# A list schedule that models VectorE's and GpSimd's shared SBUF ports and later DMA landings

## The chip, the cores and the metric

One Trainium2 chip, one core. The time is the device time of one execution in microseconds (us), the median of several runs. A run with the hardware profiler on gives the trace from which all durations here are read. The engines are called by the profile's names: PE (TensorE), PEld (its weight loads), DVE (VectorE), ACT (ScalarE), POOL (GpSimd) and SP (SyncE, which issues nearly all DMAs here).

## The reference

One layer over 4096 tokens of width 1024, batch 1. A normalised and modulated `h` feeds three groups of heads: sliding-window attention, RWKV-7 (a state that is updated token by token) and GLA (gated linear attention in chunks). Each is multiplied by its SiLU gate, and one output projection follows.

```python
h = _rmsnorm(x, g_pre) * (1.0 + scale[:, None]) + shift[:, None]
proj = h @ w_in
aq, ak, av, ag, rkv, rg, gq, gkk, gv, gg = jnp.split(proj, ...)
attn = _sliding_window_attention(...) * jax.nn.silu(ag)
rwkv = _rwkv7_mixer(...) * jax.nn.silu(rg)
gla = _gla_mixer(...) * jax.nn.silu(gg)
y = jnp.concatenate([attn, rwkv, gla], axis=-1) @ w_out
return x + gate[:, None] * _rmsnorm(y, g_post)
```

## The kernel before

The tokens are worked off in 16 chunks of 256. Weights and activations are split into a high and a low float16 part, and a projection sums three products.

**Phase 1** (from about 100 us to 1000 us of the span) runs, for each chunk: loading and normalising `x` (tiles `xh`, `xt`, `rsx`, `rb`, and the transposed activations `hT`); the projections into the PSUM tiles `pv`, `lp`, `zz`, `gqk`, through two banks that they share in turn; GLA (`qb`, `op`, `osb`, and the transposes `ot`); and RWKV. RWKV's inner triangular solve goes through small 32x32 matmuls (`Xp`, `Xq`, `X2`), its state update through a loop of four steps a chunk: `rp` on PE, a copy `rs` on DVE, `up` on PE, two copies into `UV` on ACT, `sp` on PE, and `Ss`, `Sst` on DVE. Its output `yp` is copied to `ysb`, normalised (statistics `bst`, `mv` and the small `ve` on DVE; the power `yr`, the subtraction `ysb<-ysb,mv` and the product `ysb<-ysb,yr` on POOL) and transposed (`yt`). Beside it the weights of the later phase are read in pieces `cs`, split into `ch` by ACT and DVE and written to DRAM; POOL also works out the gate's adaLN row (`gaw`, `gacc`) and masks (`ATm`).

**Phase 2** (to the end) runs the attention's projections (`kp`, `qp`, `vp`), the gates (`gp`), attention (`sc`, `pr`, `pT`, `ovp`) and the output projection, in seven products a chunk (`op`). Four of the seven weight blocks stay in SBUF (`o1`, `o4`, `o5`, `o6`); three are streamed through one tile `ov` in halves. The result `yv` gets the residual added from `x2`, whose transfer shows as `x<-in_x`.

**What sets the order.** Each operation goes through a `Lane`, which calls the real engine at line 339 (so every row of the profile carries that line) and tells an `Order` about it. `Order.note` (from line 100) records for each operation a `Step`: its engine, how long it holds the engine (`occ`), when its result is there (`lat`), and what it needs. `Order.pin` (from line 225) then does a list schedule over all recorded steps of a phase: it takes the engine that can start first, picks among that engine's ready steps the one of the lowest rank (about the order in which the program emitted it), with an exception on PE that avoids changing the array's tiling, puts it at the earliest time that the model allows, and ties it behind the last step of that engine. The model decides nothing but the order on each engine; on the chip each engine then works its queue off in that order and waits at its head for whatever is not there. `pin` is called twice, once after phase 1 and once after phase 2. The steps between (the first projections of phase 2) are left to the framework's own priorities.

In that model DVE and POOL are independent, and a DMA's result is there 1.9 to 4.8 us after its issue, by size (the line with `(8, 1.9), (32, 2.0), ...`).

Of the kernel before, what the change touches and what calls it, by code (L numbers as in the profile page):

```python
# [35 lines left out]
URGENT = 150  # L36
HOME = {('kp', 'mq'): 'tr', ('cw', 'm'): 'at'}
TILING_WAIT = 0.6
LANES = ((0.06, 1.04e-3, VL), (0.02, 1.0e-3, AL), (0.1, 2.3e-3, 0.0), (0.0, 1e-3 / 2.4, PL), (0.05, 0.0, 2.0))

SIZE = {F16: 2, BF16: 2, F32: 4, I32: 4}
# [17 lines left out]
class Step:  # L59


    __slots__ = ("ins", "eng", "occ", "lat", "table", "array", "bytes", "half", "rank", "needs", "turn", "start", "end", "then", "joint")


class Order:
# [34 lines left out]
    def note(self, eng, name, outs, ins, func, r):  # L100

        st = Step()
        st.ins, st.eng, st.table, st.array, st.bytes, st.then = r.ins, str(eng.engine).split(".")[-1], None, None, 0, []
        st.joint = self.joint
        st.half, st.rank = None, len(self.steps) + self.lag
        e, o = st.eng, outs[0]
        on_psum = [a for a in ins if str(a.tensor.space) == "PSUM"]
        n = max(math.prod(a.shape[1:]) for a in [o, *ins[:1]])
        cols = len([a for a in ins[1:] if math.prod(a.shape[1:]) == 1]) if n > 1 else 0
        if e == "PE":  # L110
            f32, lhs = ins[0].dtype == F32, self.region(ins[0])
            n = math.prod(o.shape[1:])
            _, p0, p1, _ = self.region(o)
            rows, cs = (lhs[1] // 32, (lhs[2] + 31) // 32), (p0 // 32, (p1 + 31) // 32)
            rows, cs = [(0, 4) if b - a > 2 else (a, b) for a, b in (rows, cs)]
            mode = (rows[1] - rows[0], cs[1] - cs[0])
            took = n * (2 if f32 else 1) / 2400 + 0.003
            took = max(took, 0.056 if not f32 else 0.0 if mode[1] < 4 else 0.109 if n > 16 else 0.21)
            issue = 0.017 if f32 and mode == (1, 2) else 0.009 if f32 and mode[0] == 1 else 0.007
            cells = [4 * a + b for a in range(*rows) for b in range(*cs)]  # L120
            st.array = (mode, cells, 2 if f32 and name == "matmul" else 1, took, issue)
            st.occ = st.lat = 0.0
        elif e == "SP":
            st.bytes = math.prod(ins[0].shape) * SIZE[ins[0].dtype]
            kb = st.bytes / 1024
            st.occ = 0.47
            st.lat = next((t for k, t in ((8, 1.9), (32, 2.0), (128, 2.3), (256, 2.6), (512, 3.5)) if kb <= k), 4.8)
        elif e == "Activation":
            st.occ = (0.05 if on_psum else 0.093) + 0.093 * (len(ins) - 1) + 0.832e-3 * n
            st.lat = st.occ + 0.1  # L130
            if len(outs) > 1:
                st.occ += 0.187
                st.lat = st.occ + 0.02
            st.table = LN_TABLE if func == AF.Ln else EXP_TABLE if func in (AF.Exp, AF.Tanh) else None
        elif e == "Pool":
            if name == "memset":
                st.occ = 0.06
            elif name == "tensor_copy":
                st.occ = 0.25 if n <= 2 else 0.11 + 0.95e-3 * n
            elif n <= 8:  # L140
                st.occ = 0.33 + 0.165 * n
            else:
                st.occ = 0.42 + 1.5e-3 * n if n <= 512 else 1.85e-3 * n
            st.lat = st.occ + 0.05
        else:
            if name == "tensor_reduce":
                n = math.prod(ins[0].shape[1:])
            fast = name in ("tensor_scalar", "tensor_single_scalar") and not on_psum and o.dtype == F32
            fixed, rate = 0.065 + 0.06 * (cols > 0), 1.04e-3
            if fast:  # L150
                rate = 0.53e-3
            elif name == "transpose":
                fixed = 0.09
            elif name == "tensor_tensor_scan":
                rate = 2.08e-3
            elif name == "memset":
                fixed, rate = 0.05, 0.3e-3
            elif name == "tensor_tensor" and len(o.shape) == 3 and o.shape[2] <= 16 and n > 16:
                fixed, rate = 0.09, 1.55e-3
            st.occ = fixed + rate * n  # L160
            st.lat = st.occ + 0.085

        k, st.needs, st.turn = len(self.steps), {}, []
        out_r, in_r = [self.region(a) for a in outs], [self.region(a) for a in ins]
        if e in ("Activation", "DVE"):

            st.half = (out_r[0][1], in_r[0][1] if e == "Activation" and in_r and out_r[0][2] - out_r[0][1] <= 64 else None)
        tiles = {a.tensor.name: a.tensor for a in [*outs, *ins]}

        if e == "SP" and self.behind is not None:  # L170
            st.turn.append(self.behind)

        def need(j, data=False):
            st.needs[j] = st.needs.get(j, False) or data

        for t, tensor in tiles.items():
            if t not in self.known:
                self.known.add(t)
                if t in self.held and tensor.tag:
                    held = self.slots.setdefault((tensor.owner_uid, tensor.tag), [])  # L180

                    if held and self.users.get(held[-1]):
                        st.turn.append(self.users[held[-1]][0])
                    if len(held) == self.held[t]:
                        for j in self.users.get(held.pop(0), ()):
                            need(j)
                    held.append(t)
            elif t in self.held and self.users.get(t):
                st.turn.append(self.users[t][0])
            if str(tensor.space) == "PSUM":  # L190
                for j in self.users.get(t, ()):
                    need(j)

        def meet(a, b):
            return a[1] < b[2] and b[1] < a[2] and (a[3] is None or a[3] & b[3])

        def covered(a, b):
            return b[1] <= a[1] and a[2] <= b[2] and (a[3] is None or not a[3] & ~b[3])

        for a in in_r:  # L200
            for w, j in self.wrote.get(a[0], ()):
                if meet(a, w):
                    need(j, True)
        for a in out_r:
            if a[3] is not None:
                for old in (self.wrote, self.read):
                    for w, j in old.get(a[0], ()):
                        if meet(a, w):
                            need(j)
                    old[a[0]] = [(w, j) for w, j in old.get(a[0], ()) if not covered(w, a)]  # L210
            self.wrote.setdefault(a[0], []).append((a, k))
        for a in in_r:
            self.read.setdefault(a[0], []).append((a, k))
        for t in tiles:
            self.users.setdefault(t, []).append(k)
        st.needs.pop(k, None)
        self.steps.append(st)
# [7 lines left out]
    def pin(self):  # L225

        steps = self.steps
# [16 lines left out]
                ready[st.eng][k] = 0.0  # L244
        free = dict.fromkeys(ENGINES, 0.0)
        cells, mode, table, pipe, half = [0.0] * 16, None, None, 0.0, {}
        last, count = {}, 0
        while count < len(steps):
            e = min((e for e in ENGINES if ready[e]), key=lambda e: max(free[e], min(ready[e].values())))
            now = max(free[e], min(ready[e].values())) + 1e-9  # L250
            at = sorted((k for k, t in ready[e].items() if t <= now), key=lambda k: (steps[k].rank, k))
            k = at[0]
            if e == "PE" and mode is not None and steps[k].array[0] != mode:

                same = [q for q in at if steps[q].array[0] == mode]
                wait = max(now - ready[e][q] for q in at if steps[q].array[0] != mode)
                if same and (mode != (4, 4) or wait < TILING_WAIT):
                    k = same[0]
            first = max(free[e], ready[e].pop(k))
            for k in bursts.get(k, [k]):  # L260
                st, t = steps[k], max(first, free[e])
                if e == "PE":
                    m, at, passes, took, issue = st.array
# [7 lines left out]
                else:  # L271
# [3 lines left out]
                            t = max(t, free[e] + 0.115)  # L275
                    if st.table is not None and st.table != table:
                        t, table = max(t, free[e] + 1.28), st.table
                    free[e], st.end = t + st.occ, t + st.lat
                    if st.bytes:

# [1918 lines left out]
```

## Time and profile before

| | us |
|---|---|
| median of 3 runs | 1997.24 (1992.85 to 1998.64) |
| the profiled execution | 1996.2 |
| its span in the trace | 1994.4 |

The span is divided by the engines' work. Over it PE is busy 94%, DVE 72%, ACT 56%, POOL 19%, and almost all of POOL's work is in phase 1. A row of the wait view reads: engine and tile that waited, what released it, then the sum in us, how many times, and the longest. A row of the timeline reads: start, duration, engine, operation, output and inputs, count, and in brackets the idle time before it with its releaser. A row of the grouped view ends in the group's busy time, the mean of one in ns, and the idle time before it.

### The profile page before, as it was taken

The numbers are of one execution on the slowest core, as the hardware profiler recorded it, in microseconds if no ns is written. First come the engines' busy times: TensorE is split into PE (matmuls) and PEld (weight loads), VectorE is DVE, ScalarE is ACT, GpSimd is POOL, SyncE is SP. The second block draws the span as 40 slices with busy tenths as digits, with TensorE's granted clock in tenths as the row PEclk, the third lists the DMA queues.
The fourth block names the chain that finished last, engine by engine and source line by source line (L and its number), as shares of the span: only waits on it lengthen the run. The fifth ranks groups of instructions, "written<-read, shape, count | busy, mean of one in ns | idle before, by whom it ended". The sixth has DMA issues, their size and how long they took to land.

```text
span 1994.4 us, 59065 instructions
## 1 busy us (share of the span) xinstructions
PE 1882.8 (94%) x24651; PEld 1453.4 (73%) x24651; DVE 1427.5 (72%) x3919; ACT 1115.0 (56%) x2529; POOL 373.1 (19%) x549
## 2 busy tenths in 40 slices
PE   5799989999999999999999999999999999999997
PEld 1677777777777777777776677876778767787793
DVE  4877877788877888777647776667666676666766
ACT  4877878677786676565435443344434444434443
POOL 0623223543223454223200000000000000000001
PEclk8999999999999999999999999999999999999999
DMA  9345544443342433125234433344333443334315
GB/s 373 128 152 179 155 140 125 148 139 109 105 133 88 125 111 111 61 65 185 77 132 142 151 109 112 109 146 130 109 110 109 149 130 109 100 117 151 110 47 181
DMA packets 154261, 257.55 MB, mean 129 GB/s; under 512 B 49026, under 2 KB 100994, under 8 KB 147844
## 3 DMA queue, kind: packets, MB, share of 16 engines
q1 hardware_dynamic: 153844, 253.19, 39.7%
q8 instruction: 195, 3.19, 0.7%
q14 instruction: 78, 0.64, 0.1%
q10 hardware_dynamic: 144, 0.52, 0.1%
HBM read 192.83 MB, written 60.82 MB: 127 GB/s over the span
## 4 chain that ended last, share of the span: by engine, by line
PE 55%; DVE 23%; DMA 9%; ACT 6%; issue 4%; POOL 1%; SPq 1%; ACTq 0%; DVEq 0%; POOLq 0%
PE gp L339 16%; PE op L339 11%; PE qp L339 5%; PE zz L339 4%; PE pv L339 2%; PE kp L339 2%; PE ovp L339 2%; PE lp L339 2%; DVE mtp L339 2%; DVE q L339 2%; PE sc L339 2%; DVE tsc L339 1%; SPq L339 1%; PE gqk L339 1%; DMA ov<-woscr 1%
## 5 line engine op out<-in xcount | busy, mean ns | idle before, releaser
L339 PEld LDWEIGHTS <-mtp 128*128 128x128 f16 x1344 | 128.7, 98 | 144.9 <-issue 9.2
L339 ACT ACTIVATE pr<-pr,nm,lsc 128x160 f32<-128x160 f32 (+2 forms) x256 | 129.0, 506 | 101.8 <-DVE nm L339 101.7
L339 PE MATMUL op<-o,mtp 128*128 128x512 f16 x768 | 182.2, 379 | 1.9 <-DVE yv L339 1.7
L339 PE MATMUL op<-ov,mtp 128*128 128x512 f16 x576 | 140.8, 379 | 4.4 <-DMA ov<-woscr 4.4
L339 PEld LDWEIGHTS <-hT 128*128 128x128 f16 x1536 | 117.6, 99 | 24.0 <-ACT hT L339 3.9
L339 ACT ACTIVATE ag<-gp,gh 128x512 f32<-128x512 f32 x64 | 43.9, 686 | 158.8 <-PE gp L339 158.8
L339 POOL TENSOR_TENSOR ry<-sy,expo 128x1 f32<-128x1 f32 x30 | 17.7, 606 | 584.7 <-DVE sy L339 584.7
L339 DVE SCALAR_TENSOR_TENSOR ag<-ag,gp 128x512 f32<-128x512 f32 x64 | 43.7, 683 | 103.1 <-ACT ag L339 103.1
L339 DVE TENSOR_TENSOR yv<-op,yv 128x512 f32<-128x512 f32 x105 | 72.1, 688 | 59.0 <-PE op L339 39.6
L339 PE MATMUL pv<-gvh,hT 128*128 128x272 f16 x512 | 98.2, 284 | 6.3 <-ACT hT L339 3.8
L339 PE MATMUL zz<-hT,kh 128*128 128x256 f16 x512 | 93.0, 274 | 0.0
L339 PE MATMUL zz<-hT,rh 128*128 128x256 f16 x512 | 92.5, 277 | 0.1
L339 PE MATMUL lp<-hT,Lh 128*128 128x256 f16 x512 | 91.7, 273 | 0.3 <-ACT vg L339 0.3
L339 PE MATMUL gqk<-hT,gqkh 128*128 128x256 f16 x512 | 87.9, 273 | 3.4 <-DVE zb L339 3.3
L339 DVE CUSTOM_DVE_ANT_0 pr<-sc,ab,kept 128x160 f32<-128x160 f32 (+2 forms) x256 | 83.1, 375 | 10.7 <-PE sc L339 10.2
L339 PE MATMUL gp<-hT,q4h 128*128 128x256 f16 x512 | 90.1, 276 | 0.0
L339 PE MATMUL qp<-hT,q1h 128*128 128x256 f16 x512 | 87.0, 275 | 0.9 <-DVE kT L339 0.9
L339 PE MATMUL qp<-hT,q0h 128*128 128x256 f16 x512 | 86.3, 273 | 0.5 <-issue 0.5
L339 PE MATMUL zz<-hT,vh 128*128 128x256 f16 x512 | 86.3, 273 | 0.0
L339 PE MATMUL gp<-hT,q3h 128*128 128x256 f16 x512 | 85.3, 273 | 0.0
L339 PE MATMUL gp<-hT,q5h 128*128 128x256 f16 x512 | 85.1, 273 | 0.0
L339 PE MATMUL gp<-hT,q6h 128*128 128x256 f16 x512 | 85.0, 273 | 0.0
(429 smaller groups left out, 5736.6 us busy)
## 6 DMA issues: line engine op xcount, KB each, us to landing
ov<-woscr SPq DMA_DIRECT2D x96, 512.0 KB, 4.5
xh<-in_x SPq DMA_DIRECT2D x32, 512.0 KB, 4.4
xt<-in_xc SPq DMA_DIRECT2D x16, 1024.0 KB, 8.2
hscr<-hT SPq DMA_DIRECT2D x16, 1024.0 KB, 5.0
hT<-hscr SPq DMA_DIRECT2D x16, 1024.0 KB, 5.0
x<-in_x SPq DMA_DIRECT2D x30, 512.0 KB, 4.2
out<-yv SPq DMA_DIRECT2D x30, 512.0 KB, 2.9
cs<-in_w SPq DMA_DIRECT2D x56, 256.0 KB, 3.6
```

The source lines that it names most:

```text
L339: r = f(*args, **kw)
```

## The change

The recorded step gets a flag `port`. On DVE it is set when no input is in PSUM and the operation either reads two tensors (elementwise, scan, scalar_tensor_tensor) or is a tensor_scalar or copy of at least 32 elements a partition. On POOL it is set when the operation is wider than 8 elements a partition. `pin` keeps one time `held`: a flagged step on either engine starts no earlier than `held`, and sets it to its own end. If the step that an engine would take is flagged and the ports are held for over 0.3 us more, the first ready step without the flag is taken instead. Beside that, the table of DMA landings is raised. No operation is added, removed or altered: on each engine the same instructions stand in another order, 65 table loads on ACT among them, as before.

```diff
+SWAP = 0.3
...
-            st.lat = next((t for k, t in ((8, 1.9), (32, 2.0), (128, 2.3), (256, 2.6), (512, 3.5)) if kb <= k), 4.8)
+            st.lat = next((t for k, t in ((8, 2.0), (32, 2.2), (128, 2.8), (256, 3.7), (512, 4.6)) if kb <= k), 5.2)
...
+        wide = max([math.prod(a.shape[1:]) for a in [*outs, *ins]])
+        if e == "DVE":
+            two = len(ins) > 1 and name in ("tensor_tensor", "tensor_add", "tensor_sub", "tensor_mul", "tensor_tensor_scan",
+                                            "scalar_tensor_tensor")
+            st.port = not on_psum and (two or wide >= 32 and name in ("tensor_scalar", "tensor_single_scalar", "tensor_copy"))
+        else:
+            st.port = e == "Pool" and wide > 8
...
+            if steps[k].port and held > now + SWAP:
+                k = next((q for q in at if not steps[q].port), k)
...
+                    if st.port:
+                        t = max(t, held)
+                        held = t + st.occ
```

Of the 18648 matmuls on PE, 9126 stand ahead of phase 2's first projection before and 9062 after; the number of times that neighbouring matmuls there differ in array tiling is 540 before and 538 after. Three places follow.

**ACT, around the evacuation of `pv` in the tenth chunk.** `vg` is GLA's value tile, `ch<-cs` a pass over a piece of the output weights that was just loaded, `xt` and `hT` belong to the next chunk's normalisation. Before:

```order
L339 ACTIVATE vg_9077<-pv_9079,ivgv_252 128x256
L339 ACTIVATE vg_9077<-pv_9079,ivgk1_253 128x16
L339 ACTIVATE ch_9295,wo_ss_99<-cs_9183 128x512
L339 ACTIVATE ch_9371,wo_ss_99<-cs_9297 128x512
L339 ACTIVATE vg_9077<-pv_9147,ivgv_252 128x256
L339 ACTIVATE vg_9077<-pv_9147,ivgk1_253 128x16
L339 ACTIVATE ch_9431,wo_ss_99<-cs_9373 128x512
L339 ACTIVATE ch_9490,wo_ss_99<-cs_9433 128x512
```

Of the change:

```order
L352 ACTIVATE vg_9077<-pv_9079,ivgv_252 128x256
L352 ACTIVATE vg_9077<-pv_9079,ivgk1_253 128x16
L352 ACTIVATE xt_9306<-xt_9306,sh_74,gs_73 128x256 x3
L352 ACTIVATE hT_9421<-xt_9306 128x512
L352 ACTIVATE vg_9077<-pv_9147,ivgv_252 128x256
L352 ACTIVATE vg_9077<-pv_9147,ivgk1_253 128x16
L352 ACTIVATE xt_9306<-xt_9306,sh_74,gs_73 128x256 x2
L352 ACTIVATE hT_9421<-xt_9306 128x512
```

The passes over loaded weights moved back, and the next chunk's normalisation moved ahead of them.

**PE, around GLA's transposes `ot` of the eleventh chunk.** `zz` with `vh`, `vl` is the twelfth chunk's third RWKV projection; `gqk` is the projection after it, and `pv` with `hT_11429` is the thirteenth chunk's. Before:

```order
L339 LDWEIGHTS vh_264
L339 MATMUL zz_11933<-hT_10329,vh_264 128x256
L339 MATMUL ot_11955<-first_63,osb_11762 128x128 x4
L339 LDWEIGHTS vl_265
L339 MATMUL zz_11933<-hT_10329,vl_265 128x256
```

Of the change:

```order
L352 MATMUL pv_12198<-gvh_250,hT_11429 128x272
L352 MATMUL kp_12071<-first_63,KB_11095 128x128 x4
L352 LDWEIGHTS hT_11429
L352 MATMUL pv_12273<-gvh_250,hT_11429 128x272
L352 LDWEIGHTS hT_11429
L352 MATMUL pv_12273<-gvl_251,hT_11429 128x272
L352 MATMUL ot_11955<-first_63,osb_11762 128x128 x4
```

`ot` moved back behind the rest of `zz`, all of `gqk` and the first half of the thirteenth chunk's `pv`. Counted from the chunk's last `op` matmul, 46 full-array projection matmuls stood ahead of `ot` before and 90 stand there now.

**PE in phase 2, at a streamed weight block.** `op_20386` uses the streamed tile `ov`, whose second half is loaded apart from the first; `op_20518` is the next product, with the resident block `o4`. Before:

```order
L339 MATMUL op_20386<-ov_17806,mtp_17818 128x512
L339 LDWEIGHTS mtp_17818
L339 MATMUL op_20518<-o4_17804,mtp_17818 128x512
L339 LDWEIGHTS mtp_17818
L339 MATMUL op_20386<-ov_17806,mtp_17818 128x512
```

Of the change:

```order
L352 MATMUL op_20386<-ov_17806,mtp_17818 128x512
L352 LDWEIGHTS mtp_17818
L352 MATMUL op_20518<-o4_17804,mtp_17818 128x512
L352 LDWEIGHTS mtp_17818
L352 MATMUL op_20518<-o4_17804,mtp_17818 128x512
```

Between the two halves of `ov` one matmul of the next product stood, now eight do. This repeats in each chunk of the steady part. The order at the last chunk, where `ov` is also streamed, is the same in both.

More of the change, by code (lines that the diff above doesn't have):

```diff
@@ L59 @@
 class Step:
-    __slots__ = ("ins", "eng", "occ", "lat", "table", "array", "bytes", "half", "rank", "needs", "turn", "start", "end", "then", "joint")
+    __slots__ = ("ins", "eng", "occ", "lat", "table", "array", "bytes", "half", "rank", "needs", "turn", "start", "end", "then", "joint", "port")
 class Order:
@@ L246, in pin @@
         cells, mode, table, pipe, half = [0.0] * 16, None, None, 0.0, {}
-        last, count = {}, 0
+        last, count, held = {}, 0, 0.0
         while count < len(steps):
```

## The prediction

> **What bounds the kernel now.** I read the page first, then the engines' work by stretches, then PE's waits in each stretch, and last a few microseconds of the timeline where PE waited longest.
>
> ```profile
> span 1994.4 us, 59065 instructions
> PE 55%; DVE 23%; DMA 9%; ACT 6%; issue 4%; POOL 1%; SPq 1%; ACTq 0%; DVEq 0%; POOLq 0%
> 0.00:100.00 100.00, 66.03 (x426) 39.30 (x430) 64.28 (x193) 67.44 (x124) 34.80 (x58) 0.90 0.68 250
> 100.00:1000.00 900.00, 859.48 (x13730) 690.43 (x13722) 713.18 (x2152) 622.36 (x1344) 304.44 (x441) 1.00 0.39 122
> 1000.00:1950.00 950.00, 926.02 (x10364) 710.17 (x10363) 622.80 (x1526) 411.49 (x1038) 27.90 (x45) 1.00 0.38 121
> 1950.00:1994.40 44.40, 31.30 (x143) 13.55 (x141) 27.21 (x49) 13.73 (x25) 6.01 (x6) 0.94 0.50 171
> ```
>
> The second row is the chain of waits by engine; the others are stretches with the busy time of PE, PEld, DVE, ACT and POOL. PE sets the pace in both phases: it is idle 900.00 - 859.48 = 40.5 us in phase 1 and 950.00 - 926.02 = 24.0 us in phase 2. An order cannot shorten PE's own work, and the tiling changes stay at 540 against 538, so those 64.5 us bound what the change can win from 100 to 1950 us. POOL, whose ports the change models, works 304.44 us in phase 1 and 27.90 in phase 2: the port part of the change is a matter of phase 1. The first 100 us (34 idle on PE) wait for the first transfers, and PE's order differs little there; I count nothing. So the question is which of PE's waits go, and which come.
>
> ```profile
> PE ot L339 <- DVE osb L339: 5.3, 5, 1.6
> PE gqk L339 <- DVE zb L339: 3.3, 4, 1.3
> PE Xq L339 <- DVE Xs L339: 3.1, 3, 1.7
> PE yt L339 <- POOL ysb L339: 2.6, 1, 2.6
> PE ktp L339 <- DVE bon L339: 2.6, 4, 1.1
> PE vp L339 <- DVE zb L339: 1.8, 3, 0.7
> PE zp L339 <- ACT vg L339: 1.5, 1, 1.5
> PE yt L339 <- ACT osb L339: 1.1, 2, 0.7
> PE sp L339 <- ACT UV L339: 0.7, 3, 0.3
> ...
> PE yt L339 <- POOL ysb L339: 5.3, 2, 2.6
> PE op L339 <- DMA ov<-woscr: 4.4, 5, 2.1
> ```
>
> The first nine are PE's waits between 100 and 1000 us, the last two those of the whole span. No single wait carries phase 1.
>
> **The ports, as the trace has them.** DVE and POOL do get in each other's way:
>
> ```profile
> 703.28 0.75 DVE L339 SCALAR_TENSOR_TENSOR ch<-cs,wo_sc,ch 128x512 f16<-128x512 f32 x1 [0.43 <-ACT ch L339]
> 705.76 1.55 DVE L339 SCALAR_TENSOR_TENSOR ch<-cs,wo_sc,ch 128x512 f16<-128x512 f32 x1
> 705.50 1.27 POOL L339 TENSOR_TENSOR ysb<-ysb,mv 128x512 f32<-128x512 f32 x1
> L339 DVE SCALAR_TENSOR_TENSOR ch<-cs,wo_sc,ch 128x512 f16<-128x512 f32 x24 | 21.0, 878 | 5.3 <-ACT ch L339 5.3
> L339 DVE TENSOR_TENSOR k<-k,zb 128x512 f32<-128x512 f32 x13 | 11.0, 848 | 0.5 <-ACT k L339 0.5
> L339 DVE TENSOR_TENSOR RA<-zb,ep 128x512 f32<-128x512 f32 x13 | 8.9, 681 | 0.0
> L339 DVE TENSOR_SCALAR ve<-mv 128x8 f32<-128x8 f32 x11 | 7.0, 637 | 0.0
> L339 DVE TENSOR_SCALAR og<-og 128x8 f32<-128x8 f32 x12 | 1.9, 157 | 0.0
> ```
>
> The same operation takes 0.75 us alone and 1.55 when a wide POOL operation is running. Three groups of the first 800 us give a floor for this stretch: `ch` (0.878 - 0.75) x 24 = 3.1 us, `k` against `RA` of the same size (0.848 - 0.681) x 13 = 2.2, `ve` against `og` (0.637 - 0.157) x 11 = 5.3, together 10.6 us of DVE time. The ceiling is POOL's 304 us. But DVE has slack: 713 of 900 us busy.
>
> `ve` reads 8 elements a partition, and the planner flags a tensor_scalar only from 32 on, so it still believes that `ve` is free of POOL. The 5.3 us of `ve` therefore stay in my sum. [...]
>
> **The change, term by term.**
>
> (a) `ot`. It waits for `osb`, which comes through a power on POOL and a DVE product of two SBUF tensors.
>
> ```profile
> 705.34 0.63 PE L339 MATMUL ot<-first,osb 128*128 128x128 f32 x4 [1.15 <-DVE osb L339]
> 703.37 0.27 PE L339 MATMUL zz<-hT,vl 128*128 128x256 f16 x1
> 703.48 0.38 PE L339 MATMUL zz<-hT,vh 128*128 128x256 f16 x2
> ```
>
> A projection matmul starts every 0.11 us (703.37 to 703.48). In the place shown above 46 of them covered the way from `op` to `ot`, now 90, so 44 x 0.11 = 4.8 us more cover against a wait of 1.15. Counted so over the 16 chunks, the cover rises from 750 to 866 matmuls, but unevenly: the five that waited gain 10, 13, 44, 3 and 8, or 1.1, 1.4, 4.8, 0.3 and 0.9 us, against 5.3 / 5 = 1.1 us each. As `osb` too stands further back on DVE, I take three fifths of 5.3 us: **-3.2** (ends 0 and -5.3).
>
> (b) `yt`, the same way for RWKV: from the last `yp` to `yt` 1089 projection matmuls before, 1188 now, most of it in chunks 8 to 12. The waits are 5.3 on POOL and 1.1 on ACT. Those on POOL are in the last two chunks, where the cover rises only from 31 to 33 and from 36 to 44 matmuls, 0.2 and 0.9 us. So 1.1 + 0.2 + 0.9: **-2.2** (0 to -6.4).
>
> (c) `vp`, `zp`, `ktp`, `Xq`, `gqk`: 12.3 us of waits. The matmuls move together with what they wait for: `ktp` stands as closely behind `bp`, and `Xq` behind `Xp`, as before. Only `vp` gains cover; half of its 1.8: **-0.9** (+3 to -12.3, the gain's end being the rows, the loss a quarter of them).
>
> (d) Later landings, phase 1. The old table had 2.6 us for 256 KB and 3.5 for 512 KB, the new has 3.7 and 4.6:
>
> ```profile
> cs<-in_w SPq DMA_DIRECT2D x56, 256.0 KB, 3.6
> xh<-in_x SPq DMA_DIRECT2D x32, 512.0 KB, 4.4
> AS<-adr SPq DMA_DIRECT2D x32, 64.0 KB, 2.2
> ACT ch L339 <- DMA cs<-in_w: 29.2, 16, 3.8
> ACT xh L339 <- DMA xh<-in_x: 22.0, 13, 4.5
> 551.57 0.63 ACT L339 ACTIVATE ch<-cs 128x512 f16<-128x512 f32 x1 [2.81 <-DMA cs<-in_wo]
> ```
>
> The new numbers are right for the two that ACT waits on (3.6 and 4.4 us), and too late for `AS` (2.8 against 2.2). At 551.57 ACT stood 2.81 us at the head of its queue with the second `vg` and the next chunk's `xt` behind it; the order above shows that work moved ahead. That takes up to 29.2 + 22.0 us out of ACT's idle time, but PE waited for what stood behind only as `zp` (1.5 us). I take that and half as much again for the port effect on DVE's copies, **-2.3** (0, if ACT's slack hid it all, to -10.6, the floor above, if all of DVE's stretch reached PE).
>
> (e) Phase 2, the second half of `ov`.
>
> ```profile
> 1300.11 2.75 PE L339 MATMUL op<-o,mtp 128*128 128x512 f16 x12
> 1304.23 1.46 PE L339 MATMUL op<-ov,mtp 128*128 128x512 f16 x6
> 1307.77 0.68 DVE L339 TENSOR_TENSOR yv<-op,yv 128x512 f32<-128x512 f32 x1
> PE op L339 <- DMA ov<-woscr: 2.4, 2, 2.1
> ```
>
> Such matmuls start every 0.22 us (12 take 2.75), so seven more give the transfer 1.5 us. Of the 4.4 us of waits, 2.4 are after 1950 us (last row), at the last chunk, whose order is unchanged. The other three are shorter than 1.5 us, since they add to 2.0: **-2.0** (0 to -2.0). The product's own end comes 1.5 us later, here at 1304.23 + 1.46 + 1.5 = 1307.2, and the next product but one needs its PSUM bank, which `yv` on DVE frees. DVE gets to `yv` only at 1307.77, so the delay is hidden by 0.6 us of other work on DVE; were that gone, up to 0.6 us a chunk, 8 us over 14 chunks.
>
> On DVE the residual's addition, which waited for its transfer, moves behind one gate operation; PE has no wait row for either, so nothing.
>
> (f) What is lost. In the state's loop the cover from `up` to `sp`, which hides two `UV` copies on ACT, falls from 658 to 468 projection matmuls over 64 steps: 190 x 0.11 = 20.9 us of cover. Beside it other small matmuls stand, and `sp` waited only 0.7 us in all before. I take **+2.0** (0 to +20.9), nearer to the row than to the count.
>
> Sum: -3.2 - 2.2 - 0.9 - 2.3 - 2.0 + 2.0 = -8.6 us. The profiled execution took 1996.2 us, 1.0 under the median of 1997.24; from the median I get 1997.2 - 8.6 = **1988.6 us**, 0.43% faster.
>
> **The rivals.**
>
> *Only shifted.* The recurrence moves back on PE as a whole, and the waits come back at other hops, as (c) has it for `ktp` and `Xq`. For it: the waits are many and small, and nothing of PE's work goes. Against it: `ot` and `yt` gain cover itself. Then (a) to (d) and (f) cancel and (e) stays: 1997.2 - 2.0 = 1995.2.
>
> *The loop of the state loses its cover.* Place: `up` to `sp`, 64 times. ACT now takes weight passes in the waits it had, so the `UV` copies come later, and the cover is 20.9 us smaller. If over 2.0 + 8.6 = 10.6 us of it, about half, were needed, the gain is gone; if all, 1988.6 - 2.0 + 20.9 = 2007.5. For it: the count. Against it: 0.7 us of waits before, and ACT is busy only 622 of 900 us.
>
> *The model fits so much better that half of PE's idle time in phase 1 goes.* 40.5 / 2 = 20.3, with (e): 1997.2 - 22.3 = 1974.9. For it: 23% of the chain is DVE, and ACT's 51 us of waits for DMAs. Against it: covers at most hops did not grow.
>
> **How the numbers follow.** Forecast 0.47, only shifted 0.28, lost cover 0.13, half the idle time 0.12. A difference of about 0.3% (6 us) is what a measurement of this kernel can tell from none, so the forecast (with a tenth of its weight falling within) and the last rival count as faster: 0.57; within: 0.30; slower: 0.13. The range 1970 to 2003 takes in the third rival and the bounds of (c) and (d), and leaves out most of the second.
>
> **What would show it.** Right: PE's waits of `ot` on `osb` at 2 us or so, `op` on `ov` near 2.4 in two waits, ACT's waits for `cs` and `xh` well under 51 us, `ve` still near 600 ns. Wrong: PE's waits of `sp`, `up`, `rp` at several us, or PE's idle time in phase 1 at 40 us as before with other names in the rows.

## The result, and the profile after

The changed kernel takes 1982.05 us (median of 4 runs, 1979.33 to 1984.65) beside 1997.94 for the kernel before on the same chip: ratio 0.9926, 95% interval [0.9904, 0.9948]. Measured once more, later, with more runs of both, it took 1987.1 against 1995.4: ratio 0.9949 [0.9931, 0.9967]. (One run of each kernel in that measurement, far off at 2693 and 3752 us, is left out.) So it is faster by 0.5 to 0.7%; the forecast was 0.43%.

The page's rows and the stretches of the changed kernel, as in the prediction (busy time of PE, PEld, DVE, ACT and POOL, then PE's granted clock):

```profile
span 1982.8 us, 59059 instructions
PE 58%; DVE 19%; ACT 9%; DMA 9%; issue 3%; SPq 2%; POOL 1%; DVEq 0%; ACTq 0%; POOLq 0%
0.00:100.00 100.00, 68.88 (x459) 42.59 (x460) 65.94 (x196) 69.22 (x129) 35.63 (x55) 0.91 0.69 258
100.00:1000.00 900.00, 859.21 (x13764) 691.41 (x13761) 712.57 (x2163) 618.07 (x1344) 300.26 (x443) 0.99 0.39 122
1000.00:1950.00 950.00, 930.57 (x10355) 709.51 (x10346) 627.88 (x1531) 414.23 (x1039) 27.96 (x45) 1.00 0.39 123
```

These stretches are cut by time, and the program has moved in them. It is better to cut both traces at the same matmuls: the first of `gqk`, the first of `kp` behind the product of the second output chunk, and the last pieces of the last product. First before, then after:

```profile
0.00:89.00 89.00, 58.75 (x358) 33.12 (x359) 53.55 (x169) 57.42 (x108) 30.56 (x54) 0.90 0.76 281
89.00:1087.00 998.00, 949.04 (x14829) 760.93 (x14827) 775.72 (x2320) 669.43 (x1460) 313.02 (x449) 0.99 0.39 122
1087.00:1976.30 889.30, 867.67 (x9433) 656.25 (x9433) 590.54 (x1418) 384.50 (x955) 25.62 (x43) 1.00 0.39 122
```

```profile
0.00:86.90 86.90, 57.34 (x359) 32.92 (x360) 53.36 (x169) 58.90 (x112) 27.10 (x45) 0.90 0.74 276
86.90:1080.30 993.40, 947.62 (x14830) 760.93 (x14828) 774.95 (x2320) 665.75 (x1458) 313.14 (x457) 0.99 0.40 124
1080.30:1964.40 884.10, 865.70 (x9434) 654.67 (x9433) 589.15 (x1418) 383.43 (x953) 25.69 (x43) 1.00 0.39 123
```

The start is 2.1 us shorter, phase 1 with its end 4.6, phase 2 5.2. PE's idle time (first number less PE busy) falls from 49.0 to 45.8 in the second row and from 21.6 to 18.4 in the third. The rest of the difference is PE's *busy* time, which is smaller by 1.4 to 2.0 us in each row though the same matmuls run in it. That is the first sign of something that the prediction did not have.

The trace of the second measurement, of the same program in another execution and cut at the same matmuls, shows how much of this holds:

```profile
0.00:87.30 87.30, 57.49 (x359) 33.03 (x360) 53.10 (x169) 58.77 (x111) 27.08 (x45) 0.90 0.74 275
87.30:1086.00 998.70, 952.22 (x14830) 763.62 (x14828) 774.95 (x2320) 664.97 (x1459) 312.32 (x458) 0.98 0.39 123
1086.00:1973.00 887.00, 867.19 (x9434) 655.11 (x9433) 589.14 (x1419) 383.27 (x953) 25.62 (x43) 1.00 0.39 123
```

The start is short again. Phase 1 is as long as before the change, at a lower clock and with 46.5 us of idle time; phase 2 is 2.3 us shorter, with 19.8 us of idle time.

PE's waits of the changed kernel from 100 to 1000 us (total, times, longest), and the wait for `ov` over the whole span:

```profile
PE pv L352 <- DVE zb L352: 5.1, 1, 5.1
PE ot L352 <- DVE osb L352: 3.4, 3, 1.7
PE sp L352 <- ACT UV L352: 2.9, 3, 2.3
PE yt L352 <- POOL ysb L352: 2.9, 1, 2.9
PE Xp L352 <- issue: 2.5, 1, 2.5
PE Xp L352 <- DVE D L352: 2.4, 3, 1.3
PE X L352 <- DVE Xs L352: 1.7, 1, 1.7
PE bp L352 <- ACT UV L352: 1.6, 1, 1.6
PE zp L352 <- ACT vg L352: 1.4, 2, 0.8
PE gqk L352 <- DVE zb L352: 0.8, 1, 0.8
PE op L352 <- DMA ov<-woscr: 2.4, 2, 1.9
```

`vp`, `ktp` and `Xq <- Xs` are gone from the list and `gqk` has shrunk, but `pv`, `sp`, `X` and `bp` are in their place. The names changed more than the sum did. ACT's and DVE's rows moved as the change means them to:

```profile
ACT ch L352 <- DMA cs<-in_w: 13.6, 6, 5.2
ACT xh L352 <- DMA xh<-in_x: 14.3, 8, 7.4
L352 DVE TENSOR_SCALAR ve<-mv 128x8 f32<-128x8 f32 x13 | 8.9, 684 | 0.0
L352 DVE TENSOR_TENSOR k<-k,zb 128x512 f32<-128x512 f32 x14 | 10.4, 744 | 0.0
```

ACT waits 27.9 us for the two loads instead of 51.2, and `k` on DVE takes 744 ns instead of 851 (both from 100 to 900 us); `ve`, which the planner does not know of, stays long at 684 (603 before).

### The profile page after: what moved, and what is told of

The parts are those of the page before. It is cut to its first block, busy times and chain, and to the rows that moved or that the text cites. A ratio compares the mean times of both kernels' runs of the same rounds, so it can differ in the third digit from the quotient of the medians.

```text
span 1982.8 us, 59059 instructions
## 1 busy us (share of the span) xinstructions
PE 1878.0 (95%) x24651; PEld 1451.6 (73%) x24651; DVE 1425.1 (72%) x3919; ACT 1111.7 (56%) x2529; POOL 369.9 (19%) x549
## 4 chain that ended last, share of the span: by engine, by line
PE 58%; DVE 19%; ACT 9%; DMA 9%; issue 3%; SPq 2%; POOL 1%; DVEq 0%; ACTq 0%; POOLq 0%
PE gp L352 17%; PE op L352 11%; PE zz L352 5%; PE qp L352 5%; PE kp L352 3%; PE pv L352 2%; PE lp L352 2%; PE ovp L352 2%; DVE mtp L352 2%; DVE q L352 2%; DMA AS<-adr 2%; PE gqk L352 2%; PE sc L352 2%; SPq L352 2%; DVE pr L352 1%
```

## The experiments

The theories, by the numbers that the expectations use. **1:** the landings carry the gain. **2:** the ports carry it, that is, the planner's count of DVE and POOL holding each other up (`ch` at 0.75 and 1.55 us in the prediction's rows); **2b:** phase 1 gets shorter as the planner's numbers get truer. **3, a draw:** any new order of the same operations moves the time by several us. **G, the clock:** told below, where the runs had led to it.

### One part at a time

```diff
(the kernel before, new landing table alone)
-            st.lat = next((t for k, t in ((8, 1.9), (32, 2.0), (128, 2.3), (256, 2.6), (512, 3.5)) if kb <= k), 4.8)
+            st.lat = next((t for k, t in ((8, 2.0), (32, 2.2), (128, 2.8), (256, 3.7), (512, 4.6)) if kb <= k), 5.2)
```

> The kernel before with the new landing table alone, no port model. Theory 1 (the landings carry the gain): phase 2 (POOL works 28 us there, so ports can hardly matter) ends about 5 us shorter, as in the changed kernel, the start 2 us shorter, and phase 1 part of its 4.4 us; in all 1984 to 1990 us, at least 8 us under before. ACT's waits for cs and xh (51.2 us before) go below 20. Theory 2 (the ports carry it): within 3 us of before, 1994 to 2000. Theory 3 (any new order of the same operations moves the time by several us, and the gain is a draw): anything from 1982 to 2005, and together with the ports-only kernel not additive, by 5 us or more.

Measured: 1994.5 against 1996.2, ratio 0.9989 [0.9978, 0.9999].

```diff
(the changed kernel, landing table of before)
-            st.lat = next((t for k, t in ((8, 2.0), (32, 2.2), (128, 2.8), (256, 3.7), (512, 4.6)) if kb <= k), 5.2)
+            st.lat = next((t for k, t in ((8, 1.9), (32, 2.0), (128, 2.3), (256, 2.6), (512, 3.5)) if kb <= k), 4.8)
```

> The changed kernel with the landing table of before: the port model alone. Theory 1 (landings): 1993 to 1998, phase 2 as before within 1 us, phase 1 at most 4 us shorter. DVE's mean of k<-k,zb (830 ns before, 737 in the changed kernel) and of osb<-osb,orr (796, 729) fall as in the changed kernel, since that is what the ports do. Theory 2 (ports): 1982 to 1988 with phase 1 shorter by 6 us or more. Theory 3 (a draw): anything from 1982 to 2005, and phase 2 moves too, though no port work is there.

Measured: 2005.7 against 1996.2, ratio 1.0043 [1.0028, 1.0058]: slower. Each part did its own work all the same, though ACT's two waits with the landings alone, 25.4 us, stay above the 20 that theory 1 had. ACT's rows with the landings alone, then DVE's `osb` with the ports alone (796 ns before):

```profile
ACT xh L339 <- DMA xh<-in_x: 13.6, 9, 3.7
ACT ch L339 <- DMA cs<-in_w: 11.8, 8, 2.7
L352 DVE TENSOR_TENSOR osb<-osb,orr 128x512 f32<-128x512 f32 x16 | 11.6, 727 | 0.0
```

So -1.7 and +9.5 us stand against -15.9 and -8.3 for both together. The parts do not add; theories 1 and 2 fall.

### How much does a new order as such do?

```diff
(the kernel before, nudged)
-            ... (256, 2.6), (512, 3.5)) ...
+            ... (256, 2.55), (512, 3.45)) ...
(the changed kernel, nudged)
-            ... (256, 3.7), (512, 4.6)) ...
+            ... (256, 3.75), (512, 4.65)) ...
```

> The kernel before with the landings of 256 KB and 512 KB lowered by 0.05 us each, which no argument could value: it measures what a new order as such does. Theories 1 and 2: within 2 us of before (1995 to 1999). Theory 3 (a draw): away from before by 4 us or more, to either side.

Measured: 1999.6 against 1996.2, ratio 1.002 [1.001, 1.003].

> The changed kernel with the landings of 256 KB and 512 KB raised by 0.05 us each (3.75 and 4.65). Theories 1 and 2: within 2 us of the changed kernel, 1980 to 1985. Theory 3 (a draw): 4 us or more away from 1982, to either side, and then more likely slower.

Measured: 1989.1 against 1996.2, ratio 0.9964 [0.995, 0.9977], 2 to 7 us over the unnudged change. One or two hundredths of a landing time, which no argument could value, moves the kernel before by 3.4 us (2 to 6 by the interval): more than theories 1 and 2 allowed, a little less than the 4 us of theory 3. The nudge of the changed kernel tells less, since that kernel's own two measurements lie 5 us apart. So theory 3 has something.

### Phase 2 alone

```diff
+            new = ((8, 2.0), (32, 2.2), (128, 2.8), (256, 3.7), (512, 4.6), (1e9, 5.2))
+            old = ((8, 1.9), (32, 2.0), (128, 2.3), (256, 2.6), (512, 3.5), (1e9, 4.8))
+            st.lat = next(t for k, t in (new if self.pinned else old) if kb <= k)
...
-        steps = self.steps
+        steps, self.pinned = self.steps, True
```

> The kernel before with the new landing table for the steps of phase 2 alone; the order of phase 1 stays that of before, the order of phase 2 on PE becomes that of the changed kernel. Theory 1, as the forecast's term (e) had it: 2 to 3 us under before (1993.2 to 1994.2 if before stands at 1996.2), since the part from the second output-projection chunk on took 889.3, 889.3 and 887.8 us in three profiles with the old order and 884.1 and 888.1 in two with the new. Theory 3 (every new order is a draw of several us, phase 2 too): 4 us or more from before to either side.

Measured: 1994.8 against 1995.3, ratio 0.9999 [0.9987, 1.0011], that is from -2.6 to +2.2 us. By the names in the two traces, the order of phase 2 is here that of the changed kernel on DVE, ACT and POOL, and on PE but for a few small `ovp` matmuls among each other. The 4 us of theory 3 are excluded, and so is at least half of the 5.2 us that phase 2 had gained in the profile: that part was this one execution, not the order. PE's rows over the whole span, first before, then of this run (the wait for `ov` before is 4.4 us):

```profile
PE op L339 <- DVE yv L339: 1.7, 8, 0.6
PE op L342 <- DMA ov<-woscr: 3.0, 2, 2.4
PE op L342 <- DVE yv L342: 2.6, 13, 0.6
```

The wait for `ov` falls by 1.4 us, and the wait for the bank that `yv` frees rises by 0.9. The prediction had seen this second wait and taken it as hidden.

### The planner's numbers made truer

```diff
(the changed kernel, narrow operations flagged too)
-            st.port = not on_psum and (two or wide >= 32 and name in ("tensor_scalar", ...))
+            st.port = not on_psum and (two or wide >= 2 and name in ("tensor_scalar", ...))
```

> The changed kernel with tensor_scalar and copies flagged as users of the shared ports from 2 elements a partition on, so that the planner knows that ve (627 ns against og's 157) is held up. Theory 2b (phase 1 gets shorter as the model gets truer): at or under the changed kernel, 1976 to 1983, ve under 400 ns. Theory 3 (phase 1 is a draw for every order, with 5 to 6 us of spread about a mean 1 to 3 us over before): 1985 to 2000, with no bearing of whether ve got shorter.

Measured: 1990.0 against 1995.3, ratio 0.9971 [0.9953, 0.9989]. The edit works on `ve` (684 ns from 100 to 900 us in the changed kernel), and buys no time:

```profile
L352 DVE TENSOR_SCALAR ve<-mv 128x8 f32<-128x8 f32 x13 | 3.4, 263 | 0.0
```

```diff
(the changed kernel)
-            ... (128, 2.8) ...
+            ... (128, 2.2) ...
```

> The changed kernel with the landing of the class up to 128 KB at 2.2 instead of 2.8 us, as AS has it in the trace (2.3). Theory 2b: at or under the changed kernel, 1978 to 1983. Theory 3: 1985 to 2000.

Measured: 1988.2 against 1995.3, ratio 0.9962 [0.9949, 0.9974]. Neither of the two is at or under the changed kernel, so theory 2b falls. Beside that kernel's second measurement of 1987.1 they are 3 and 1 us longer, less than its own two measurements differ: they show no gain, and no clear loss.

```diff
(the changed kernel)
-SWAP = 0.3
+SWAP = 99.0
```

> The changed kernel with SWAP at 99, so that the planner counts the time that an operation waits for the ports but never picks another one for it. Theory 2b (the pick is half of the port model): half of the gain over the landings alone goes, 1986 to 1990. Theory 3: 1985 to 2000, as likely above 1994 as below.

Measured: 2008.8 against 1995.3, ratio 1.0061 [1.0045, 1.0078]: over every range that was written down for it.

### What the draw is made of

The kernels differ not only in time but in the granted clock of their runs (0.984 for the slowest; 0.990 and 0.987 for the changed kernel in its two measurements). The clock records of the traces show why. Four steps of 3.4 us of the kernel before around its wait at 1635 us (in each row the length, the busy time of PE, PEld, DVE, ACT and POOL, and PE's clock), and PE's timeline there:

```profile
1630.20:1633.70 3.50, 3.50 (x130) 3.14 (x129) 2.17 (x6) 0.69 (x1) 1.04 (x2) 1.00 0.01 5
1633.70:1637.10 3.40, 1.80 (x107) 1.53 (x91) 3.28 (x5) 1.20 (x4) 0.00 (x0) 1.00 0.37 139
1637.10:1640.50 3.40, 3.40 (x19) 2.42 (x17) 0.72 (x1) 0.00 (x0) 0.00 (x0) 0.50 0.55 180
1640.50:1643.90 3.40, 3.40 (x33) 3.05 (x32) 0.82 (x2) 0.69 (x1) 0.00 (x0) 1.00 0.61 188
```

```profile
1636.64 0.27 PE L339 MATMUL gp<-hT,q4l 128*128 128x256 f16 x1 [1.60 <-issue]
1636.74 0.38 PE L339 MATMUL gp<-hT,q4h 128*128 128x256 f16 x2
1637.45 0.42 PE L339 MATMUL gp<-hT,q4l 128*128 128x256 f16 x1
1637.66 0.64 PE L339 MATMUL gp<-hT,q4h 128*128 128x256 f16 x2
```

A step in which PE was idle for 1.60 us is followed by one at exactly half the clock: 19 matmuls instead of 33, and two of them in 0.64 us instead of 0.38. The step ahead of it was not idle as a whole: PE was busy for 1.80 of its 3.40 us. After 3.4 us the clock is full again. Half a step, 1.7 us, is lost behind a wait of 1.6. The steps form a grid: the half-clock stretches of this trace between 90 and 1970 us begin at 97.70, 947.62, 974.92 and 1637.11 us, each 3.413 us long and 249, 8 and 194 times 3.413 us apart, and those of the changed kernel at 144.81 (two steps long), 390.57, 697.77 and 933.29 us, 72, 90 and 69 times 3.413 us apart. The changed kernel has no such step in phase 2, which is most of its 2.0 us less of busy time there. In phase 1 it has five by the clock records, where before had three, so PE's work should have taken longer there, and it took 1.4 us less. Take half of PE's busy time inside the half-clock steps off (an estimate from the clock records; the ends of matmuls are modelled in these traces): PE's work in phase 1 is then 944 us before, and 940 and 938 in the two traces of the change. Counted so over the whole span, the eight traces of orders with both parts of the change lie at 1863 to 1868 us, the five others at 1869 to 1871. So the new orders shorten PE's own work at full clock by some 4 us. The number of tiling changes is nearly the same (540 and 538) and does not explain it; what does stays open.

The half-clock steps by themselves, with PE's waits of ten sizes made by VectorE (`burst(n)` is n full matmuls into one PSUM tile, `gap(p, e)` VectorE work on e elements that reads this tile and writes what the next matmul needs):

```diff
+    for e in (64, 256, 448, 640, 832, 1024, 1280, 1536, 1792, 2304):
+        for r in range(16):
+            gap(burst(40 + 5 * r % 16), e)
+    for between in (4, 20):
+        for r in range(16):
+            gap(burst(40 + 5 * r % 16), 448)
+            gap(burst(between), 448)
```

> None of the decoder is computed: bursts of 40 to 55 full matmuls (128x512, 9 to 12 us) with PE waits between them made by VectorE, ten sizes from about 0.7 to 3 us, sixteen of each, then pairs of waits of about 1 us, 4 or 20 matmuls apart; the output is a copy of a part of x. Theory G (PE's clock is judged in steps of 3.41 us, and a step with PE idle for 1.6 us or more, in one wait or several, gives a next step at half the clock; read from the traces of the decoder, where every such step of 3.4 us between 90 and 1970 us stands behind a step with at least 1.60 us of idle time): no half-clock step for waits under 1.5 us; for a wait of g between 1.6 and 3.2 us the wait falls far enough into one step with a chance of 1 - (3.2 - g) / 3.41, so about 9 of 16 at 1.7 us, 10 of 16 at 2.0, 13 of 16 at 2.5, 15 of 16 at 3.0; for pairs of 1 us, 4 matmuls apart, about 4 of 16, and none for pairs 20 matmuls apart. Rival (only a step that is idle as a whole counts): no half-clock step for any of them. [...]

Measured, in stretches of sixteen waits of one size (length, PE, PEld, DVE and POOL busy, PE's clock); the last row but one has the pairs that are 4 matmuls apart, the last those 20 apart:

```profile
729.90:918.40 188.50, 166.59 (x761) 74.22 (x761) 19.90 (x32) 0.00 (x0) 1.00 0.00 1
918.40:1110.10 191.70, 166.59 (x761) 74.28 (x761) 23.10 (x32) 0.00 (x0) 1.00 0.00 0
1110.10:1323.60 213.50, 180.07 (x760) 77.62 (x760) 30.85 (x48) 0.00 (x0) 0.94 0.00 0
1323.60:1539.70 216.10, 178.39 (x761) 77.23 (x761) 35.13 (x48) 0.00 (x0) 0.94 0.00 0
1539.70:1765.30 225.60, 179.59 (x760) 77.51 (x760) 42.89 (x64) 0.00 (x0) 0.94 0.00 0
1765.30:2018.20 252.90, 194.22 (x761) 81.05 (x761) 54.91 (x80) 0.00 (x0) 0.88 0.00 0
2018.20:2236.10 217.90, 186.35 (x825) 81.20 (x825) 27.50 (x64) 0.00 (x0) 0.98 0.00 1
2236.10:2505.80 269.70, 238.18 (x1080) 105.32 (x1080) 27.51 (x64) 0.00 (x0) 1.00 0.00 1
```

Length less PE busy, by sixteen, is the wait: 1.37, 1.57, 2.09, 2.36, 2.88 and 3.67 us. Up to 1.57 the clock is full throughout (1.00 in each of the four smaller sizes too). At 2.09 us PE's busy time for the same matmuls rises from 166.6 to 180.1: 13.5 us in 8 half-clock steps, 1.7 each. The steps counted in the clock records are 8, 7, 8 and 18 for the four larger sizes, 2 for the close pairs, none for the wide ones. The two are the point of the pairs: no wait of 1 us alone brought such a step, two in one step of the grid did. The rival, that only a wholly idle step counts, would have had no step at 2.09 us, and it falls. G's shares were too high (8, 7 and 8 of 16 where 10 to 15 were expected, 2 pairs where 4 were), so its line of 1.6 us was too low here: put into its own formula, the counts at 2.09, 2.36 and 2.88 us give lines of 1.9, 2.1 and 2.3 us (an estimate from these counts and steps of 3.41 us). One such step in full: from 1118.72 to 1122.14 us PE was busy for 1.33 and idle for 2.09 us, in the step after it ran 10 matmuls at 0.50 of the clock, and in the next 18 at 1.00. In the decoder the line is less sharp. In the traces of before and of the change the seven steps at full clock that brought on half clock between 100 and 1970 us had 1.60 to 3.41 us of idle time, but one with 1.95 us (from 1012.50 us, before) and one with 1.85 (from 970.88, the change) brought none. A step already at half clock kept the next one there with less, 0.60 us (from 144.81 us, the change), so the 1.60 us that the expectation had read from the traces does not hold for every step. The decoder's steps hold other, smaller matmuls, and what these count for was not tried.

So **in these runs a wait of PE cost its length, and 1.7 us more when some 2 us of idle time (in the decoder 1.60 us or more in the seven steps above) fell into one step of a grid that does not start with the program.** In the trace of before its steps begin 2.12 us after the start of the span, in that of the change 1.45 us. The two traces of the change, 1982.8 and 1991.3 us long with mean clocks of 0.989 and 0.986, have 5 and 10 half-clock steps between 90 and 1970 us, so at least five of the ten stand at places of their own. Five more at 1.7 us would be 8.5 us; of the 8.5 us between the two, PE's busy time has 6.2 and its idle time 2.3.

### The draw, with the clock taken out

Time multiplied by the mean clock of the run is an estimate of what a kernel would take at full clock (the start and the end are in it too, with a clock of 0.90 and 0.84 before and of 0.90 and 0.77 in the changed kernel). Three last kernels were to tell whether that number goes with the parts of the change:

> The changed kernel as it is, once more beside the others. Theory G (time is PE's waits plus half-clock steps that some of them bring): time times mean clock 1960 to 1966 as the first time (1982.0 x 0.990 = 1962), the time itself 1980 to 1988. Theory 3 (its order is one lucky draw that repeats): 1980 to 1985 again, 4 us or more under its neighbours (1988.2, 1989.1, 1990.0).

```diff
(the changed kernel; the second kernel has the 3.75 and 4.65 us of the nudge as well)
-SWAP = 0.3
+SWAP = 0.1
...
-SWAP = 0.3
+SWAP = 99.0
```

> The changed kernel with SWAP at 0.1 instead of 0.3: another order with both parts of the change and the pick. Theory G with a real share of the model: time times mean clock 1962 to 1967, as in the four orders with both parts so far (1962.2, 1964.7, 1965.1, 1965.5), time 1982 to 1994 by the clock it gets. Theory 3: time times clock anywhere from 1962 to 1978.

> The changed kernel with SWAP at 99 (no pick) and the landings of 256 KB and 512 KB raised by 0.05 us: another order without the pick. Theory G with a real share of the model: time times mean clock 1973 to 1979, as without the pick (1976.3) and as in the kernel before (1975.1 to 1976.0); the time by the clock, 1992 to 2011. Theory 3: time times clock anywhere from 1962 to 1978, and 1966 or less would tell against the pick's share.

All kernels (median, ratio to the kernel before, mean clock of the runs, and the mean of time x clock):

| kernel | us | ratio [95%] | clock | us x clock |
|---|---|---|---|---|
| before (three times) | 1995.3 to 1996.2 | | 0.990 | 1975.1 to 1976.2 |
| before, nudged | 1999.6 | 1.002 [1.001, 1.003] | 0.989 | 1978.3 |
| landings alone | 1994.5 | 0.9989 [0.9978, 0.9999] | 0.988 | 1970.4 |
| landings in phase 2 | 1994.8 | 0.9999 [0.9987, 1.0011] | 0.989 | 1972.8 |
| ports alone | 2005.7 | 1.0043 [1.0028, 1.0058] | 0.986 | 1976.0 |
| both, no pick | 2008.8 | 1.0061 [1.0045, 1.0078] | 0.984 | 1976.3 |
| both, no pick, nudged | 1999.5 | 1.002 [1.0011, 1.0029] | 0.985 | 1969.9 |
| both, pick at 0.1 | 2003.0 | 1.0033 [1.002, 1.0046] | 0.985 | 1972.7 |
| both, narrow flagged | 1990.0 | 0.9971 [0.9953, 0.9989] | 0.987 | 1964.7 |
| both, 128 KB at 2.2 | 1988.2 | 0.9962 [0.9949, 0.9974] | 0.989 | 1965.5 |
| both, nudged | 1989.1 | 0.9964 [0.995, 0.9977] | 0.988 | 1965.1 |
| **the change**, first time | 1982.1 | 0.9926 [0.9904, 0.9948] | 0.990 | 1962.2 |
| **the change**, second time | 1987.1 | 0.9949 [0.9931, 0.9967] | 0.987 | 1961.7 |

The change gives the same 1962 both times. What differs between its two measurements, 5 us, is the clock. The 9.5 us that the ports alone lose and the 13.5 that the missing pick loses are the clock too: 1976 in the last column, as before. The landings alone are 5.6 us under their own measurement of before in this column, the landings in phase 2 alone 2.3, near term (e), which the clock took back. But the last two expectations of G failed: with the pick at 0.1 the number is 1972.7 where 1962 to 1967 was expected, and without the pick, nudged, 1969.9 where 1973 to 1979 was. So the parts of the change do not fix the number. Orders with both parts and the pick lie from 1962 to 1973 (the mean of the five is 1966), the seven others, the one before among them, from 1970 to 1978 (mean 1974). About 8 of the 14 us at full clock may be put down to the change, by these means; the rest would be this one order's luck. The two groups overlap, with twelve orders in all, so the share is not settled. No version beat the change, and none was built to keep PE's waits under 2 us.

## Why the prediction was right, and where it was not

The sign and the range hold: 1982.05 and 1987.1 lie in 1970 to 2003. The forecast of 1988.6 was 1.5 us from the second measurement and 6.6 from the first, and that it came so near is in good part luck: one order gave both times, and the terms of the sum mostly did not come as written. Of the signs of being right, `ov` in two waits, ACT's shorter waits and the long `ve` came, and `ot` at 2 us or so did not. A sign of being wrong came too: from 100 to 1000 us PE is idle for 900.00 - 859.21 = 40.8 us, as before, with other names in the rows. By the prediction's terms:

- **(a) `ot`**, forecast -3.2: its wait for `osb` went from 5.3 to 3.4 us, three waits instead of five, -1.9. But two waits of `ot` with other releasers stand beside it now, `rn` 1.2 and `winv` 0.4, which were not there before. In all, `ot` waits 5.0 us instead of 5.3, and 5.3 in the second trace: more cover moved the waits and hardly shortened them.
- **(b) `yt`**, forecast -2.2: from 100 to 1000 us 2.6 + 1.1 became 2.9, -0.8. What `yt` waits for on POOL did not shrink (over the whole span 5.3 became 5.6), and that is where the covers had risen by no more than 0.9 us.
- **(c) the hops that seemed to move together**, forecast -0.9: here the term was mis-sized. Of 12.3 us, 1.4 (`zp`) and 0.8 (`gqk`) are left, 10 us went, of which `X` and `Xp`, the neighbours of `Xq` in the solve, took 2.7 back. The step "the matmuls move together with what they wait for" looked at the order at one or two hops and took it for all.
- **(d) later landings in phase 1**, forecast -2.3: ACT's waits fell as foreseen (51.2 to 27.9) and PE's row for it, `zp`, did not (1.5 to 1.4). The run with the landings alone had the same fall on ACT and won 1.7 us in all. So ACT's slack hid most of it, near the lower end of the term.
- **(e) phase 2**, forecast -2.0: PE's waits for `ov` are 2.4 us in two, to the tenth as written; in the second trace they are 4.2 in two, so the tenth was luck. The wait for `yv`, which the prediction took as hidden by 0.6 us of other work on DVE, rose from 1.7 to 3.3 us in 14 waits (2.6 in 13 in the second trace). Alone the term measured -0.5 us, with an interval that holds both 0 and -2.0.
- **(f) the state's loop**, forecast +2.0: `sp` waits 2.9 us for `UV` instead of 0.7, +2.2. With `bp`, `yp` and `atp`, which now wait for `UV` too, it is 5.8 us instead of 0.7 (5.3 in the second trace), so +2.0 was too small. The second rival's large loss did not come.
- **What no term had.** New waits came at other hops, the longest at `pv`, which waits 5.1 us for `zb`. Behind it stand two half-clock steps, from 144.8 to 151.6 us. DVE had stood 4.08 us before it for `rn`, and ACT, which makes `rn`, is busy 11.94 of the 12.00 us from 130 to 142 (below, ACT's busy time is the fourth of the five). Two weight passes are among ACT's work there, but no run took them away, so that they cause the wait is not shown. In the kernel before the same `rn` came 5 us later, and `pv` hardly waited, since PE came to it later still. PE's order ran further ahead than what it waits for. PE's idle time from the first `gqk` to the end of phase 1 fell by 3.2 us only, and by 2.5 in the second trace, so the rival *only shifted* describes PE's waits in phase 1 better than the sum of its rows. The start, counted at nothing, gave 2.1.

```profile
130.00:142.00 12.00, 10.16 (x94) 8.39 (x93) 7.79 (x22) 11.94 (x23) 1.37 (x5) 1.00 0.64 203
139.92 0.88 DVE L352 SCALAR_TENSOR_TENSOR rn<-zb,kkh,rn 128x256 f32<-128x256 f32 x2 [4.08 <-ACT rn L352]
145.25 0.39 PE L352 MATMUL pv<-gvh,hT 128*128 128x272 f16 x1 [5.09 <-DVE zb L352]
145.04 0.88 DVE L339 SCALAR_TENSOR_TENSOR rn<-zb,kkh,rn 128x256 f32<-128x256 f32 x2 [1.66 <-ACT rn L339]
150.43 0.28 PE L339 MATMUL pv<-gvh,hT 128*128 128x272 f16 x1 [0.34 <-DVE zb L339]
```

- **`ve`** stays long (684 ns from 100 to 900 us, 603 before), as the prediction had it. The run with narrow operations flagged gives no sign that its 5.3 us of DVE time were on PE's path; other DVE rows grew in it, `RA<-zb,ep` from 691 to 756 ns.

Two assumptions under all the terms failed. One is that an order cannot shorten PE's own work: by the estimate above it fell by some 4 us at full clock, a term of the size of the largest in the sum, put at nothing. The other is that a wait of PE costs its length. With the half-clock steps it did not: eight of the sixteen waits of 2.09 us brought a step that cost 1.7 us more, and none of the sixteen pairs of waits of 1 us that lay 20 matmuls apart did. This second one did not make the gain: the two traces that were compared first, of before and of the change, have four and five such steps. It is what parts the change's two measurements, and what the ports alone and the missing pick lose. The prediction quoted PE's clock for four stretches (0.90, 1.00, 1.00, 0.94) and read nothing from it.

## What to carry to other kernels

Before a change of order is priced by hops, nudge a number that cannot matter and time it: here that alone moved the kernel before by 3.4 us, about the size of the largest terms in the sum. Where PE sets the pace, as here with 94% of the span, look at the longest single waits first, and at the granted clock beside them: here sixteen pairs of waits of 1 us, 20 matmuls apart, brought no half-clock step, and sixteen single waits of 2.09 us brought eight, of 1.7 us each. A planner's numbers made truer move its order, and only as far as the order's waits are on the path do they move the time; judge such an edit by several neighbouring orders, not by one.

## What was not expected of the hardware

- PE's clock fell to half for a step of 3.4 us after some 2 us of idle time in the step before (8 of 16 waits of 2.09 us, none of 96 waits of up to 1.57 us; in the decoder one wait of 1.60 us did it). Each such step cost 1.7 us, nearly as much as the wait behind which it came.
- The steps do not follow from the program alone: two executions of the change had 5 and 10 of them and traces of 1982.8 and 1991.3 us, 0.4% apart.
- `tensor_scalar` on 8 elements a partition is held up by POOL as well, as the prediction had read from the trace: `ve` took 684 ns on the mean where the planner was told nothing, 263 where it was told. In the kernel before, seven of the sixteen took about 0.16 us and nine 0.67 to 1.05. Each of the nine began 0.05 to 0.41 us after a POOL operation on `ysb` (eight) or `cs` (one) that was still running; at 193.20 us `ve` takes 1.00 us beside a `ysb<-ysb,mv` that runs from 193.12 for 1.05. Of the seven, four began within 0.03 us of the start of a `ysb<-ysb,mv`, two ran beside `orr<-og,expo`, and one, at 362.96, with no POOL operation.
